# Cross-attention's keys computed in the mixer's end, and its values with the memory's tokens on partitions

## The chip, the cores and the metric

The kernel runs on one NeuronCore of one Trainium2 chip. The metric is the time of one execution on the device in microseconds (us). The program holds TensorE (PE; its weight loads are listed apart as PEld), VectorE (DVE), ScalarE (ACT), a little GpSimd (POOL), and DMA transfers that the SyncE queue (SP) issues.

## The reference

A decoder trunk of two layers, sequence 512, width 1024, with a memory of 256 tokens. Each layer adds to `h` in turn: half a SwiGLU feed-forward; a mixer of 8 stick-breaking heads (width 64) and 4 gated delta-rule heads (width 128) with one input and one output projection; a read of the memory; and half a SwiGLU again. The change touches the end of the mixer and the read of the memory:

```python
def memory_cross_attention(xn, memn, w_q, w_kv, w_o):
    q = (xn @ w_q).reshape(B, S, 4, 256)
    k, v = jnp.split(memn @ w_kv, 2, axis=-1)      # memn: 256 x 1024
    ...
    s = jnp.einsum('bshd,bmhd->bhsm', q, k) * (256 ** -0.5)
    p = jax.nn.softmax(s, axis=-1)
    o = jnp.einsum('bhsm,bmhd->bshd', p, v).reshape(B, S, D)
    return o @ w_o
```

`memn` is `rms_norm(mem, mem_norm[l])`: the memory is the same in both layers, only the gain differs. The keys and values therefore depend on nothing that the layer computes.

## The kernel before

All activations lie transposed, with 128 features on the partitions and 512 tokens (for the memory 256) along a row. Every dense product is made from three fp32r matmuls: an operand is split into a high part (a cast on ACT, `split_act`, L170) and a low part (a subtraction on DVE, `split_low`, L176), and `mm3` (L234) issues high x high, high x low and low x high. One matmul here includes its weight load.

**Weights.** A weight block is 128 output features by 1024 inputs, 512 KB. `load` (L179) brings it into one of three raw buffers over SP's queue, `unit` (L186) splits it into one of four pairs of buffers (`W_BUFS`). `self.plan` is the list of blocks in the order in which they are used, `xattn_plan` (L1280) and its like write it, and `take` (L211) takes the next and has the ones after it loaded and split ahead, as far as the four buffers go. `products` (L239) multiplies a block with an operand in eight steps, a `yield` after each.

**Order.** The order of TensorE's instructions is written by hand: stages are Python generators that `weave` (L92) runs against a planned clock. `self.clk` grows with each matmul by its planned time, a `yield 1200.0` says that the thread's next step is due 1200 ns later, and `yield ("q3",)` that it waits for a mark set by another thread. Of the threads that are due, the first in the list goes on. Waits at this level only set the order; on the chip an instruction waits for the data that it needs. The other engines' order comes from a scheduler that also goes by the program's order and by priorities.

**The mixer** (L1150) weaves four threads: the norm's statistics, the delta-rule heads one after another (`mixer_gdn`, `gdn_head` L966), the stick-breaking pairs one after another (`mixer_sb`, `sb_pair` L827), and the dense products (`mixer_dense`, L1183), which fill in wherever no chain step is due. A delta-rule head is a chain of small matmuls, each followed by a DVE step: seven levels of a triangular inverse (their masked product on DVE is L1079, their updates L1084 and L1088), then four chunks of the state (DVE at L1102, L1108, L1118). The dense thread makes the projections of all heads, then four blocks for the gate `z` (L1207 to L1209), then the output projection `project_out` (L690): its first two pairs of blocks take the first four operands (the stick-breaking pairs, `turned`), the fourth of which waits for `sb3`, the last pair's end; then `gated` (L1218) transposes the delta-rule heads' outputs and multiplies them with the gate, and the remaining steps follow.

**The cross-attention** (`xattn`, L1284) loads the memory (`load_mem`, L1258), scales and splits it (`mem_operands`, L1265), and weaves the norm, the heads, and `xattn_dense` (L1291): 8 key blocks, 8 value blocks, 8 query blocks, then the output projection. A key or value block is 24 matmuls with 128 output features on the partitions and 256 tokens along the row. The keys are multiplied by the memory's rms factor along the row (`self.mb`, L1300). The attention needs the values with tokens on the partitions, so each value block is multiplied (L1316), transposed by two TensorE transposes, and copied by ACT (L1307).

Of the kernel before, what the change touches and what calls it, by code (L numbers as in the profile page):

```python
# [30 lines left out]
KD = D // P  # L31
# [16 lines left out]
G_F1, G_MX, G_XA, G_ME, G_F2, G_SB, G_GD, G_CV, G_AL, G_DT, G_LAYER = (  # L48
    0, 8, 16, 24, 32, 40, 44, 45, 93, 97, 101)
# [3 lines left out]
class Trunk:  # L53
# [125 lines left out]
    def load(self, src):  # L179

        raw = self.wpool.tile([P, KD * P], F32, tag="wraw", name=self.name("wraw"), bufs=3)
        raw = raw[:, :src.shape[1]]
        self.nc.sync.dma_start(raw, src)
        return raw
# [781 lines left out]
    def gdn_head(self, layer, head):  # L966
        nc = self.nc
# [4 lines left out]
        q, k, v = self.qkv[head]  # L972
# [102 lines left out]
        for n in range(len(small), len(LEVELS)):  # L1075
            yield 500.0 if n > len(small) else 3300.0
            b = gd()
            each(b, lt, Y)
            tt(v3(U), v3(b), many(mask(n)), op=ALU.mult)  # L1079
            yield 1200.0  # L1080
            if n < len(LEVELS) - 1:
                b = gd()
                each(b, X, U)
                tt(Y, Y, b, op=ALU.subtract)  # L1084
                yield 0
            b = gd()
            each(b, U, X)
            tt(X, X, b, op=ALU.subtract)  # L1088
        rho = self.rsqrt_log(sq4, NT, "rq")
        nc.vector.tensor_scalar(out=rho, in0=rho, scalar1=P ** -0.5, scalar2=None, op0=ALU.mult)  # L1090

# [47 lines left out]
        on = self.on[head] = self.slot(f"s{4 + head}")  # L1139
        tt(v3(on), v3(o), wide(ro), op=ALU.mult)  # L1140
        self.mark(f"g{head}", 5400.0)

    @staticmethod
    def mixer_plan(wi, wo):
# [38 lines left out]
    def mixer_dense(self, layer, x):  # L1183
        nc = self.nc
        wg = self.gate_weights(layer)
        early = yield from self.products(1, x, self.AT[:1])
        b = self.bank("dense", self.AT[1:2])
        for k, (xh, xl) in enumerate(x):
            parts = [(b[:16, :], wg[:, k, :], xh), (b[:8, :], wg[:, k, 0:8], xl)]
            for i, (o, l, r) in enumerate(parts if k == 0 else parts[::-1]):  # L1190
                self.mm(o, l, r, start=k + i == 0, stop=True, skip_group_check=k + i > 0)
            yield 200.0
        self.ab16 = self.slot("s14", shape=(16, S))
        nc.scalar.copy(self.ab16, b[:16, :])
        early.append((yield from self.project(x)))
        yield ("rb",)
        self.mark("ab")
        for p in range(4):
            if p >= 2:
                yield (f"q{p - 2}",)  # L1200
            yield from self.gdn_project(layer, p, x, early if p == 0 else [])
            if p >= 2:
                yield (f"qk{p - 2}",)
            yield from self.sb_project(p, x)
        yield ("qk2",)
        z = self.sb([P, 4, S], "qk", bufs=2)
        for p in range(4):  # L1207
            ps = yield from self.project(x)
            nc.vector.tensor_tensor(z[:, p, :], ps, self.rb, op=ALU.mult)  # L1209
        last = nc.scalar.activation(z, z, AF.Silu)  # L1210
        self.exp_set(last)
        ops = []

        def turned(p):
            yield (f"sb{p}",)
            ops.append(self.to_x(p, self.sbo[p]))

        def gated():  # L1218
            for p in range(4):
                yield (f"g{p}",)  # L1220
                b = self.bank("gate", ("b4", "b5"))
                self.transposes(b, self.on[p])
                t = self.slot(self.turn("gz", ("s12", "s2")))
                nc.vector.scalar_tensor_tensor(out=t, in0=b, scalar=self.gain(layer, G_GD),
                                               in1=z[:, p, :], op0=ALU.mult, op1=ALU.mult)
                ops.append(self.to_x(4 + p, t))

        yield from self.project_out(ops, [turned(p) for p in range(4)], "sb3", gated())


    def mem_norm(self):

        nc = self.nc
        yield ("last",)
        acc = self.cv[:, 4:]
        for i in range(4):
            t = self.slot(("s33", "s6")[i % 2])
            nc.sync.dma_start(t.rearrange("p (k m) -> p k m", k=2), self.a["memT"][:, 2 * i:2 * i + 2, :])
            dst = t if i else acc
            nc.scalar.activation(dst, t, AF.Square)  # L1240
            if i:
                nc.vector.tensor_tensor(acc, acc, t, op=ALU.add)
# [8 lines left out]
        mt = self.rsqrt(ms, 2, "mn")  # L1251
# [6 lines left out]
    def load_mem(self):  # L1258
        mem = self.sb([P, 4, S], "qk", bufs=2)
        for i in range(4):  # L1260
            self.nc.sync.dma_start(mem[:, i, :].rearrange("p (k m) -> p k m", k=2),
                                     self.a["memT"][:, 2 * i:2 * i + 2, :])
        return mem

    def mem_operands(self, layer):  # L1265
        nc = self.nc
        mem = self.load_mem()
        x = []
        for k in range(KD):
            if k % 2 == 0:  # L1270
                mh, ml = self.slot(f"s{k // 2}", F32R), self.slot(f"s{4 + k // 2}", F32R)
            cs = slice((k % 2) * M, (k % 2 + 1) * M)
            g = self.gain(layer, G_ME, k)
            nc.scalar.activation(mh[:, cs], mem[:, k // 2, cs], AF.Copy, scale=g)
            nc.vector.scalar_tensor_tensor(out=ml[:, cs], in0=mem[:, k // 2, cs], scalar=g,
                                           in1=mh[:, cs].bitcast(F32), op0=ALU.mult, op1=ALU.subtract)
            x.append((mh[:, cs], ml[:, cs]))
        return x

    @staticmethod  # L1280
    def xattn_plan(wq, wkv, wo):
        return [*(wkv[i] for i in range(2 * KD)), *(wq[i] for i in range(KD)), *(wo[i] for i in range(KD))]

    def xattn(self, layer):  # L1284
        self.begin()
        mem = self.mem_operands(layer)
        x = self.norm(layer, G_XA, ("s24", "s25", "s26"))
        self.kt, self.vm, self.q, self.xo = {}, {}, {}, []
        self.weave(self.rms(self.GD, 8000.0, 9000.0), self.xattn_heads(), self.xattn_dense(mem, x))

    def xattn_dense(self, mem, x):  # L1291

        nc = self.nc
        kv4 = self.sb([P, 4, S], "qk", bufs=2)
        room = [self.slot(f"s{i}") for i in (34, 35, 36)] + [kv4[:, i, :] for i in range(4)] + [self.slot("s39")]
        for i in range(KD):
            if i % 2 == 0:
                kt = self.kt[i // 2] = room[i // 2]
            ps = yield from self.project(mem, M, self.MM + self.AT[:2])
            nc.vector.tensor_tensor(kt[:, (i % 2) * M:(i % 2 + 1) * M], ps[:, :M], self.mb, op=ALU.mult)  # L1300
        vf = None

        def turned(i, vf):
            b = self.bank("turn", ("b4", "b5"))
            self.transposes(b, vf, n=2)
            dst = self.vm[i // 2].rearrange("p (m d) -> p m d", m=2)[:, :, (i % 2) * P:(i % 2 + 1) * P]
            nc.scalar.copy(dst, b[:, :M].rearrange("p (m d) -> p m d", m=2))  # L1307

        for i in range(KD):
            if i % 2 == 0:  # L1310
                self.vm[i // 2] = room[4 + i // 2]
            ps = yield from self.project(mem, M, self.MM + self.AT[:2])
            if i:
                turned(i - 1, vf)
            vf = self.slot(self.turn("vf", ("s31", "s32")))
            nc.vector.tensor_tensor(vf[:, :M], ps[:, :M], self.mb, op=ALU.mult)  # L1316
        for i in range(KD):
            if i >= 4 and i % 2 == 0:
                yield (f"sc{i // 2 - 2}",)
            ps = yield from self.project(x, banks=(("b0", "b7", "b1")[i % 3],))  # L1320
            if i == 0:
                turned(KD - 1, vf)
# [179 lines left out]
```

## Time and profile before

| | |
|---|---|
| median of 3 runs | 2451.75 us (2449.06 to 2458.12) |
| the profiled execution | 2449.16 us |
| its span in the profile | 2447.3 us |
| TensorE busy, share of the span | 2389.6 us, 98% |
| VectorE busy | 1774.0 us, 72% |
| ScalarE busy | 1184.8 us, 48% |
| mean DMA rate | 90 GB/s |
| TensorE's granted clock, mean | 0.994 |

Busy times overlap, since the engines work side by side. TensorE's matmuls are pipelined and their ends are modelled, so the distance from one matmul's start to the next one's is the better measure of what one costs; a row of the timeline that says `x16` holds sixteen of them. "Idle before <- releaser" is the time in which an engine stood still before a group of instructions, and the instruction whose end let it go on. PEclk is the share of TensorE's full clock (2.4 GHz) that was granted; 0.5 is 1.2 GHz.

In layer 0 of the profiled execution the mixer's gate blocks end at about 630 us, its output projection's remaining steps run from 665 to 710 us, the cross-attention's keys and values from 710 to 759 us; layer 1 follows the same course some 1210 us later.

### The profile page before, as it was taken

The numbers are of one execution on the slowest core, as the hardware profiler recorded it, in microseconds if no ns is written. First come the engines' busy times: TensorE is split into PE (matmuls) and PEld (weight loads), VectorE is DVE, ScalarE is ACT, GpSimd is POOL, SyncE is SP. The second block draws the span as 40 slices with busy tenths as digits, with TensorE's granted clock in tenths as the row PEclk, the third lists the DMA queues.
The fourth block names the chain that finished last, engine by engine and source line by source line (L and its number), as shares of the span: only waits on it lengthen the run. The fifth ranks groups of instructions, "written<-read, shape, count | busy, mean of one in ns | idle before, by whom it ended". The sixth has DMA issues, their size and how long they took to land.

```text
span 2447.3 us, 36463 instructions
## 1 busy us (share of the span) xinstructions
PE 2389.6 (98%) x14580; PEld 2111.7 (86%) x14580; DVE 1774.0 (72%) x3146; ACT 1184.8 (48%) x2044; POOL 8.1 (0%) x19
## 2 busy tenths in 40 slices
PE   9999999999899999999999999999998999999998
PEld 7999987888689889898889999788886988899997
DVE  7868677888775578585686767598986655777765
ACT  5535355665544445353444444465564444444443
POOL 0000000000000000000000000000000000000000
PEclk9999999999999999999999999999999999999999
DMA  4323242111133123232323232321111422232322
GB/s 160 116 78 128 79 130 69 52 53 52 44 121 121 54 84 114 85 121 87 113 77 121 87 119 80 113 70 44 52 52 36 154 97 76 78 113 86 114 89 82
DMA packets 65273, 220.51 MB, mean 90 GB/s; under 512 B 7376, under 2 KB 10192, under 8 KB 65104
## 3 DMA queue, kind: packets, MB, share of 16 engines
q1 hardware_dynamic: 64672, 217.82, 26.9%
q8 instruction: 114, 1.87, 0.3%
q14 instruction: 55, 0.45, 0.1%
q10 hardware_dynamic: 432, 0.37, 0.1%
HBM read 216.07 MB, written 2.10 MB: 89 GB/s over the span
## 4 chain that ended last, share of the span: by engine, by line
PE 86%; DVE 11%; ACT 1%; issue 1%; DMA 1%; SPq 0%; ACTq 0%; DVEq 0%; POOL 0%
PE b L118 85%; PE b L738 1%; DVE wlo L177 1%; DVE qkv L951 1%; DVE s L865 1%; DVE s L860 1%; ACT whi L172 1%; DVE s L867 0%; DVE s L1079 0%; DVE s L177 0%; DVE s L415 0%; DMA s<-csr 0%; DVE s L1048 0%; DVE s L1088 0%; DMA wraw<-f1i 0%
## 5 line engine op out<-in xcount | busy, mean ns | idle before, releaser
L118 PE MATMUL b<-s,whi 128*128 128x256 f32 (+1 forms) x3064 | 657.3, 305 | 1.8 <-DVE s L459 1.4
L172 ACT CAST whi<-wraw 128x1024 fp32r<-128x1024 f32 (+3 forms) x412 | 387.5, 952 | 495.0 <-PE b L118 452.2
L118 PE MATMUL b<-xh,whi 128*128 128x512 f32 (+1 forms) x1552 | 582.3, 400 | 5.8 <-ACT xh L172 3.0
L118 PE MATMUL b<-xl,whi 128*128 128x512 f32 x1472 | 547.0, 392 | 4.3 <-DVE xl L299 2.4
L177 DVE TENSOR_TENSOR wlo<-wraw,whi 128x1024 fp32r<-128x1024 f32 (+3 forms) x412 | 450.8, 1101 | 123.6 <-ACT whi L172 122.1
L118 PEld LDWEIGHTS b<-s,whi 128*128 128x128 f32 x3064 | 496.9, 190 | 29.2 <-DVE s L459 1.7
L118 PE MATMUL b<-xh,wlo 128*128 128x512 f32 (+1 forms) x1288 | 503.8, 391 | 4.1 <-DVE wlo L177 4.1
L118 PE MATMUL b<-s,wlo 128*128 128x256 f32 (+1 forms) x1532 | 466.8, 305 | 1.1 <-DVE wlo L177 1.1
L118 PEld LDWEIGHTS b<-xh,whi 128*128 128x128 f32 x1552 | 291.8, 189 | 61.1 <-ACT xh L172 4.2
L118 PEld LDWEIGHTS b<-xl,whi 128*128 128x128 f32 x1472 | 277.7, 189 | 59.3 <-DVE xl L177 5.0
L118 PEld LDWEIGHTS b<-s,wlo 128*128 128x128 f32 x1532 | 291.2, 190 | 14.3 <-DVE wlo L177 1.5
L118 PEld LDWEIGHTS b<-xh,wlo 128*128 128x128 f32 x1288 | 242.8, 189 | 58.5 <-DVE wlo L177 6.9
L118 PE MATMUL b<-qk,whi 128*128 128x256 f32 (+1 forms) x1152 | 232.9, 289 | 0.0
L574 DVE SCALAR_TENSOR_TENSOR h<-b,h 128x512 f32<-128x512 f32 (+1 forms) x98 | 66.3, 679 | 176.6 <-PE b L118 176.6
L118 PEld LDWEIGHTS b<-qk,whi 128*128 128x128 f32 x1152 | 180.4, 191 | 2.4
L118 PE MATMUL b<-qk,wlo 128*128 128x256 f32 (+1 forms) x576 | 166.4, 289 | 0.0
L118 PE MATMUL b<-qkv,whi 128*128 128x256 f32 x816 | 160.4, 281 | 0.0
L172 ACT CAST whi<-vv 128x1024 fp32r<-128x1024 f32 x68 | 71.5, 1051 | 133.3 <-issue 71.4
L118 PEld LDWEIGHTS b<-qkv,whi 128*128 128x128 f32 x816 | 126.1, 190 | 0.2 <-ACT s L531 0.2
L118 PE MATMUL b<-qkv,wlo 128*128 128x256 f32 x408 | 114.7, 281 | 0.0
L118 PEld LDWEIGHTS b<-qk,wlo 128*128 128x128 f32 x576 | 110.1, 191 | 1.3
L118 PEld LDWEIGHTS b<-s,s 128*128 128x128 f32 x656 | 83.0, 191 | 25.7 <-DVE s L1079 10.5
(274 smaller groups left out, 3118.0 us busy)
## 6 DMA issues: line engine op xcount, KB each, us to landing
wraw<-f2i SPq DMA_DIRECT2D x88, 512.0 KB, 3.2
wraw<-f1i SPq DMA_DIRECT2D x86, 512.0 KB, 3.2
wraw<-wi SPq DMA_DIRECT2D x56, 512.0 KB, 3.2
wraw<-f1o SPq DMA_DIRECT2D x32, 512.0 KB, 3.5
wraw<-xkv SPq DMA_DIRECT2D x32, 512.0 KB, 3.2
wraw<-f2o SPq DMA_DIRECT2D x32, 512.0 KB, 3.5
wraw<-wo SPq DMA_DIRECT2D x16, 512.0 KB, 3.2
wraw<-xq SPq DMA_DIRECT2D x16, 512.0 KB, 3.3
```

What stands on the lines that cost most here:

```text
L118: self.nc.tensor.matmul(out, lhsT, rhs, **kw)
L172: self.nc.scalar.copy(hi, src)
L177: self.nc.vector.tensor_tensor(lo, src, hi.bitcast(F32), op=ALU.subtract)
L574: stt(out=h, in0=p, scalar=0.5, in1=h, op0=ALU.mult, op1=ALU.add)
L738: self.nc.tensor.transpose(out, src, self.ident[:src.shape[0], :src.shape[0]])
L860: nc.vector.scalar_tensor_tensor(out=t1, in0=z[:, :w], scalar=0.0, in1=t1, op0=ALU.max, op1=ALU.add)
L865: nc.vector.tensor_tensor_scan(out=run[:, back], data0=self.ones[:, 0:1].to_broadcast([P, width]), data1=t1[:, back], initial=0.0, op0=ALU ...
L951: nc.vector.scalar_tensor_tensor(out=y, in0=cv[:, 1 + i:1 + i + S], scalar=w[i], in1=y, op0=ALU.mult, op1=ALU.add)
```

## The change

**Keys.** The 8 key blocks of the weight list are put ahead of the 8 blocks of the mixer's output projection. In `mixer_dense`, four quarters of the memory are loaded one after the other into the one buffer `cv`, the first when `qk2` is marked, and each is scaled and split (`mem_operands(layer, i)`, now one quarter, into room that is free at this point) after a gate block. The last quarter is split after the mark `qk3`. Six of the eight steps of the first two key blocks come before `qk3`; the rest of the key blocks follow, with the operands of the stick-breaking pairs 0 to 2 prepared in between, and the fifth and the seventh block wait, before their result is stored, for the marks `l3` (new: the last head's levels are done) and `q3` (its chunks are done), since they go into buffers that the chain uses until then. Only then does the output projection start. The keys' multiplication and the last quarter's split have high priority with the scheduler.

**Values.** The value weights are the moving operand now and the memory the stationary one: the product comes out with 128 tokens on the partitions and 4 x 128 features along the row, so the transposes and the multiplication ahead of them go. A load fetches 256 inputs of four blocks (runs of 1 KB), and the factor of the rms, now one per partition, goes into ACT's copy.

The core of the diff:

```diff
     def load(self, src):
         raw = self.wpool.tile([P, KD * P], F32, tag="wraw", name=self.name("wraw"), bufs=3)
+        if len(src.shape) == 3:
+            self.nc.sync.dma_start(raw.rearrange("p (i c) -> p i c", i=src.shape[1]), src)
+            return raw
...
+        self.mark(f"l{head}")
         rho = self.rsqrt_log(sq4, NT, "rq")
...
         yield ("qk2",)
+        self.load_mem(0)
         z = self.sb([P, 4, S], "qk", bufs=2)
         for p in range(4):
             ps = yield from self.project(x)
             nc.vector.tensor_tensor(z[:, p, :], ps, self.rb, op=ALU.mult)
+            if p < 3:
+                self.mem_operands(layer, p)
...
-                t = self.slot(self.turn("gz", ("s12", "s2")))
+                t = self.slot(self.turn("gz", ("s2", "s3")))
...
-        yield from self.project_out(ops, [turned(p) for p in range(4)], "sb3", gated())
+        gens = [self.products(1, self.mem, self.MM, M, kn=KD) for _ in range(2)]
+        for gen in gens:
+            for _ in range(KD - 2):
+                next(gen)
+                yield 0
+        yield ("qk3",)
+        with self.tc.high_priority():
+            self.mem_operands(layer, 3)
+        self.kt = {}
+        yield from self.keys(range(2), self.MM, gens)
+        for p in range(3):
+            yield from turned(p)
+        yield from self.keys(range(2, self.KEYS), self.MM, free={4: "l3", 6: "q3"})
+        early = [self.until()] * 3 + [turned(3)]
+        yield from self.project_out(ops, early, "sb3", gated())
...
+    def load_mem(self, i):
+        self.nc.sync.dma_start(self.cv[:, 4:].rearrange("p (k m) -> p k m", k=2),
+                               self.a["memT"][:, 2 * i:2 * i + 2, :])
+
+    def mem_operands(self, layer, i):
...
+        raw = self.cv[:, 4:]
+        mh, ml = self.mem_room[2 * i:2 * i + 2]
+        for j in range(2):
+            cs = slice(j * M, (j + 1) * M)
+            g = self.gain(layer, G_ME, 2 * i + j)
+            nc.scalar.activation(mh[:, cs], raw[:, cs], AF.Copy, scale=g)
+            nc.vector.scalar_tensor_tensor(out=ml[:, cs], in0=raw[:, cs], scalar=g,
                                            in1=mh[:, cs].bitcast(F32), op0=ALU.mult, op1=ALU.subtract)
+            self.mem.append((mh[:, cs], ml[:, cs]))
+        if i < 3:
+            self.load_mem(i + 1)
+
+    def keys(self, blocks, banks, begun=(), free={}):
+        for i in blocks:
+            ps = yield from (begun[i] if i < len(begun) else self.products(1, self.mem, banks, M))
+            if i % 2 == 0:
+                if i in free:
+                    yield (free[i],)
+                self.kt[i // 2] = self.slot(("", "s13", "s34", "s35")[i // 2]) if i else self.cv[:, 4:]
+            with self.tc.high_priority():
+                self.nc.vector.tensor_tensor(self.kt[i // 2][:, (i % 2) * M:(i % 2 + 1) * M], ps[0][:, :M], self.mb,
+                                             op=ALU.mult)
+
+    def xattn_plan(self, wq, wkv, wo):
+        self.plan[-KD:-KD] = [wkv[i] for i in range(self.KEYS)]
+        wv = [wkv[KD + 4 * h:KD + 4 * h + 4, :, 2 * P * i:2 * P * (i + 1)].rearrange("i p c -> p i c")
+              for h in range(2) for i in range(KD // 2)]
+        return [*(wkv[i] for i in range(self.KEYS, KD)), *wv, *(wq[i] for i in range(KD)), *(wo[i] for i in range(KD))]
...
+        yield from self.keys(range(self.KEYS, KD), self.MM + self.AT[:2])
+        for h in range(2):
+            ps = [self.bank("dense", self.MM + self.AT[:2]) for _ in range(2)]
+            for i in range(KD // 2):
+                hi, lo = (t.rearrange("p (i c) -> p i c", i=4) for t in self.take())
+                for k in (2 * i, 2 * i + 1):
+                    cs = slice((k % 2) * P, (k % 2 + 1) * P)
+                    for m, p in enumerate(ps):
+                        ms = slice(m * P, (m + 1) * P)
+                        self.mm3(p.rearrange("p (i c) -> p i c", i=4), (mem[k][0][:, ms], mem[k][1][:, ms]),
+                                 (hi[:, :, cs], lo[:, :, cs]), k == 0, k == KD - 1)
+                    yield 0
+                self.held -= 1
+            for j in range(2):
+                vm = self.vm[2 * h + j] = kv4[:, 2 * h + j, :]
+                for m, p in enumerate(ps):
+                    nc.scalar.activation(vm[:, m * M:(m + 1) * M], p[:, j * M:(j + 1) * M], AF.Copy,
+                                         scale=self.mt[:, m:m + 1])
```

`KEYS` is 8, so all keys are made in the mixer and the `keys` call in the cross-attention makes none. What the values' new loop replaces is the pair of loops of `xattn_dense` over keys and values, with `turned`.

## Rows read from the trace of the kernel before

**Rows 1.** The page: busy time by engine, and the chain that ended last, by engine.
```profile
PE 2389.6 (98%) x14580; PEld 2111.7 (86%) x14580; DVE 1774.0 (72%) x3146; ACT 1184.8 (48%) x2044; POOL 8.1 (0%) x19
...
PE 86%; DVE 11%; ACT 1%; issue 1%; DMA 1%; SPq 0%; ACTq 0%; DVEq 0%; POOL 0%
```
**Rows 2.** Stretches: start:end, length, busy us by engine (instructions), PEclk, DMA share, GB/s.
```profile
core 0: us, PE busy (x) PEld busy (x) DVE busy (x) ACT busy (x) POOL busy (x), PEclk, DMA share, GB/s
570.70:599.50 28.80, 28.26 (x169) 24.39 (x168) 23.99 (x43) 17.38 (x32) 0.00 (x0) 1.00 0.16 56
606.00:636.10 30.10, 28.80 (x168) 23.90 (x168) 25.78 (x54) 20.06 (x33) 0.00 (x0) 1.00 0.15 53
636.10:665.10 29.00, 20.05 (x128) 17.07 (x127) 20.21 (x48) 14.07 (x38) 0.00 (x0) 0.89 0.12 37
665.10:674.00 8.90, 8.88 (x30) 6.88 (x31) 0.69 (x1) 0.00 (x0) 0.00 (x0) 0.78 0.01 2
1846.90:1874.90 28.00, 18.57 (x129) 15.66 (x128) 20.24 (x49) 14.13 (x38) 0.00 (x0) 0.92 0.11 38
...
710.30:759.50 49.20, 49.20 (x415) 49.20 (x416) 33.12 (x54) 23.67 (x32) 0.00 (x0) 1.00 0.50 172
```
**Rows 3.** Timeline of TensorE, mixer's end, layers 0 and 1 (start, us, idle before).
```profile
639.53 1.13 PE L118 MATMUL b<-s,s 128*128 128x128 f32 x8 [0.54 <-DVE s L1073]
641.88 3.10 PE L118 MATMUL b<-s,s 128*128 128x128 f32 x24 [1.22 <-DVE s L1079]
...
662.52 1.09 PE L738 MATMUL b<-cst,s 128*128 128x128 f32 x4 [1.89 <-DVE rot L264]
665.12 0.80 PE L118 MATMUL b<-xh,whi 128*128 128x512 f32 x1 [1.52 <-ACT xh L172]
...
669.26 0.39 PE L118 MATMUL b<-xh,whi 128*128 128x512 f32 x1
...
673.81 0.39 PE L118 MATMUL b<-xh,wlo 128*128 128x512 f32 x1
674.04 1.03 PE L738 MATMUL b<-cst,s 128*128 128x128 f32 x8
...
1874.89 0.80 PE L118 MATMUL b<-xh,whi 128*128 128x512 f32 x1 [1.51 <-ACT xh L172]
...
1884.70 1.03 PE L738 MATMUL b<-cst,s 128*128 128x128 f32 x8
```
**Rows 4.** Timeline of TensorE, mixer, 604.8 to 612.0 us.
```profile
605.13 0.39 PE L118 MATMUL b<-cb 128*128 128x512 bf16 x1
605.42 0.63 PE L738 MATMUL b<-cst,s 128*128 128x128 f32 x4
...
609.91 1.95 PE L118 MATMUL b<-qkv 128*128 128x128 f32 x16
611.69 0.22 PE L118 MATMUL b<-cb 128*128 128x128 bf16 x1
```
**Rows 5.** Chain that ended last, in order of time, among the value blocks (start, us).
```profile
741.05 2.87 PE b L118 x24
...
744.14 2.85 PE b L118 x24
```
**Rows 6.** Groups by line and form, 636 to 775 us (busy, mean ns, idle before).
```profile
L177 DVE TENSOR_TENSOR wlo<-wraw,whi 128x1024 fp32r<-128x1024 f32 x26 | 31.5, 1222 | 14.8 <-ACT whi L172 14.8
L172 ACT CAST whi<-wraw 128x1024 fp32r<-128x1024 f32 x26 | 26.9, 1050 | 43.5 <-PE b L118 42.2 <-issue 1.3
...
L1274 ACT ACTIVATE s<-qk,gn 128x256 fp32r<-128x256 f32 x8 | 3.6, 501 | 3.7 <-DMA qk<-memT 2.7 <-DVE xl L177 1.0
L1275 DVE SCALAR_TENSOR_TENSOR s<-qk,gn,s 128x256 fp32r<-128x256 f32 x8 | 3.5, 476 | 0.0
...
L1300 DVE TENSOR_TENSOR s<-b,mb 128x256 f32<-128x256 f32 x6 | 2.5, 422 | 0.8 <-PE b L118 0.8
L1307 ACT COPY qk<-b 128x256 f32<-128x256 f32 x6 | 2.2, 366 | 0.0
```
**Rows 7.** DMA issues, 636 to 646 us (KB each, us to landing).
```profile
qk<-memT SPq DMA_DIRECT2D x4, 256.0 KB, 5.2
```

More of the change, by code (lines that the diff above doesn't have):

```diff
@@ L1141, in gdn_head @@
         self.mark(f"g{head}", 5400.0)
+    KEYS = 8
     @staticmethod
@@ L1250, in mem_norm @@
                                 op0=ALU.mult, op1=ALU.add)
-        mt = self.rsqrt(ms, 2, "mn")
+        mt = self.mt = self.rsqrt(ms, 2, "mn")
         yield 7000.0
@@ L1256, in mem_norm @@
         nc.scalar.copy(self.mb, b[:, :M])
[L1258 to L1265, printed above, removed]
-        nc = self.nc
[L1267 to L1275, printed above, removed]
-                                           in1=mh[:, cs].bitcast(F32), op0=ALU.mult, op1=ALU.subtract)
-            x.append((mh[:, cs], ml[:, cs]))
-        return x
@@ L1280, in xattn_plan @@
-    @staticmethod
-    def xattn_plan(wq, wkv, wo):
-        return [*(wkv[i] for i in range(2 * KD)), *(wq[i] for i in range(KD)), *(wo[i] for i in range(KD))]
+    def load_mem(self, i):
+        self.nc.sync.dma_start(self.cv[:, 4:].rearrange("p (k m) -> p k m", k=2),
+                               self.a["memT"][:, 2 * i:2 * i + 2, :])
+    def mem_operands(self, layer, i):
+        nc = self.nc
+        if i == 0:
+            t = self.sb([P, 3, S], "qkv", F32R, bufs=2)
+            self.mem = []
+            self.mem_room = [t[:, 0, :], t[:, 1, :], t[:, 2, :], self.sb([P, S], "vl", F32R),
+                             self.sb([P, S], "ml", F32R), self.slot("s12", F32R)]
+        if i == 3:
+            self.mem_room += [self.slot("s14", F32R), self.sb([P, 4, S], "qk", F32R, bufs=2)[:, 0, :]]
+        raw = self.cv[:, 4:]
[5 more added lines that the diff above has]
+            nc.vector.scalar_tensor_tensor(out=ml[:, cs], in0=raw[:, cs], scalar=g,
+                                           in1=mh[:, cs].bitcast(F32), op0=ALU.mult, op1=ALU.subtract)
+            self.mem.append((mh[:, cs], ml[:, cs]))
+        if i < 3:
+            self.load_mem(i + 1)
@@ L1284, in xattn @@
+    def xattn_plan(self, wq, wkv, wo):
[3 more added lines that the diff above has]
+        return [*(wkv[i] for i in range(self.KEYS, KD)), *wv, *(wq[i] for i in range(KD)), *(wo[i] for i in range(KD))]
     def xattn(self, layer):
         self.begin()
-        mem = self.mem_operands(layer)
         x = self.norm(layer, G_XA, ("s24", "s25", "s26"))
-        self.kt, self.vm, self.q, self.xo = {}, {}, {}, []
@@ L1289, in xattn @@
-        self.weave(self.rms(self.GD, 8000.0, 9000.0), self.xattn_heads(), self.xattn_dense(mem, x))
+        self.vm, self.q, self.xo = {}, {}, []
+        self.weave(self.rms(self.GD, 8000.0, 9000.0), self.xattn_heads(), self.xattn_dense(self.mem, x))
     def xattn_dense(self, mem, x):
@@ L1294, in xattn_dense @@
         kv4 = self.sb([P, 4, S], "qk", bufs=2)
[L1295 to L1316, printed above, removed]
+        yield from self.keys(range(self.KEYS, KD), self.MM + self.AT[:2])
[16 more added lines that the diff above has]
+                                         scale=self.mt[:, m:m + 1])
         for i in range(KD):
@@ L1320, in xattn_dense @@
             ps = yield from self.project(x, banks=(("b0", "b7", "b1")[i % 3],))
-            if i == 0:
-                turned(KD - 1, vf)
             j = i % 4
```

## The prediction

> **What bounds the kernel now.** I read the page first: TensorE is busy 98% of the span and carries 86% of the chain of work that ended last [rows 1], so time is saved only by giving TensorE less to do or by filling its gaps. Then the stretches: TensorE, VectorE (DVE) and granted clock around the places that the diff touches [rows 2]. In the middle of the mixer (570.70 to 599.50) TensorE is busy 28.26 of 28.80 us. In the mixer's end (636.10 to 665.10) it is busy 20.05 of 29.00 us, and the granted clock falls to 0.89 there and to 0.78 in the 8.9 us behind it; layer 1 shows the same at 1846.90. The cross-attention's keys and values (710.30 to 759.50) fill TensorE wholly. Third, the timeline of TensorE in the mixer's end [rows 3]: from 636.10 on nothing is left for it but the steps of the last delta-rule head and the last stick-breaking pair, each waiting for DVE, until the fourth step of the output projection starts at 665.12.
>
> How much of the 29.0 us is real work? Busy time does not tell, since ends are modelled. The stretch holds 128 matmuls [rows 2]; 88 of them are 128x128 in fp32, and sixteen of those in a row take 1.78 us from start to start [rows 4], 0.111 each; the rest run from 2 to 512 columns, and I take the same mean. That is 14.2 us of work and **14.8 us of gaps**; in layer 1 28.0 less 14.2, 13.8 us. After the gaps TensorE runs at 1.2 GHz: the 30 matmuls of 512 columns from 665.12 to 674.04 take 8.92 us, where at 2.4 GHz a matmul takes 0.2275 us (20 from 669.26 to 673.81 [rows 3]), 6.83 us in all. So the low clock costs 2.1 us in layer 0. Layer 1's thirty take from 1874.89 to 1884.70, 9.81 us [rows 3], so 3.0 us. A perfect filler could win 16.9 and 16.8 us.
>
> **The change, part by part**, each per layer.
>
> Keys. 8 blocks of 24 matmuls of 256 columns leave the cross-attention for the mixer's end. 24 of them take 2.87 us [rows 5], 0.1195 each: 192 cost 22.9 us, out of a place where TensorE is full, into one that can absorb up to 16.8 us.
>
> Values. 192 matmuls of 256 columns (22.9 us) and 16 transposes (a block repeats after 3.09 us and its matmuls take 2.87 [rows 5], so 0.22 for two, 1.7 us in all) go. In come 96 matmuls of 512 columns, two weight loads where there were four: 96 x 0.2275 = 21.8 us. That wins 2.8 us.
>
> At the row the price of a weight load shows nowhere: 256 columns at 2.4 GHz alone are 0.107 us, and load and matmul together repeat after 0.1195 [rows 5]. The Trainium skill, "TensorE: Matmul & The Clock Gate", Part 3, The mechanism, has weight loads overlap running matmuls only in other row groups, and its section LDWEIGHTS prices one at columns over 1.2, here 107 ns; by that, 96 loads fewer would win about 10 us more in each layer, an estimate from that page. The trace disagrees, and the sum goes by the rows.
>
> New in the values: the moving operand is read in four runs of 128 columns, 256 apart. The trace of before shows no such fp32r matmul. Nearest rows: contiguous, 0.2275; and the mask row of the delta rule, a bf16 operand read four times over in runs of 128, which takes 0.29 us until the next starts [rows 4], some of it a change of type. I take 0.2275 (the output stays contiguous and each run is long) and keep 0.29, 6 us a layer, as the upper end; a gain is excluded, since nothing runs faster than contiguous.
>
> Other engines, in the mixer's end. DVE gets 8 splits of a weight block (1.22 us each), 8 multiplications of the keys (0.42) and 8 splits of the memory (0.48) [rows 6]: 17 us; ACT 8 casts of a block (1.05) and 8 of the memory (0.50): 12.4 us. Six of the eight memory splits lie in the z stage, where DVE is busy 25.78 of 30.10 us [rows 2], so 2.9 us just fit; the rest, 14 us, goes to the tail, where DVE has 20.2 of 29.0 us and almost nothing in the 9 us after. About 35 us of DVE work in some 44 us is 79%; in the mixer's middle it lives with 24.0 of 28.8 us, 83% [rows 2]. So DVE is not the bound by amount, but the chain's steps queue behind 1.22 us splits. In the middle that costs TensorE 0.5 us in 28.8 [rows 2], with fillers of three matmuls of 512 columns, 0.68 us; the keys' steps are 0.36 us, so a chain's step comes up sooner and waits oftener. Ends: 0.5 us a layer (as in the middle) and 9.8 (all eight splits land in the chain's way). I take 3.5, nearer the middle, whose mix it is.
>
> DMAs. Four loads of the memory (256 KB, 5.2 us to land [rows 7]) move to the z stage, into a single buffer, so SP stops at each until the quarter before it is split; queued behind it are weight loads. Three raw buffers and four split ones cover it, 5.5 us of z matmuls (24 x 0.2275) each; without that cover a load costs its 5.2 us. The value weights come in runs of 1 KB where it was 4 KB; the stretch uses half the DMA engines' time [rows 2], and blocks are loaded ahead during the output projection. Both at nothing, and the POOL queue is not touched.
>
> New waits. "qk3", "l3" and "q3" stop only the dense thread, which holds nothing else then; by the planner's own times it has keys left at each of them (about 15 us of filler fit between z and "q3"). In the values, one counter hands out the four banks: in layer 0 the second half gets b0 and b1, and the first query block needs b0, which waits for three copies of 0.37 us [rows 6] and a hand-over, about 1.4 us, after 0.3 at the start; in layer 1 the first value block waits 0.9 us for the projection's last bank. 1.2 a layer, between 0 and 1.7. The scaling of the values moves from DVE to the copies on ACT, which were there before: nothing.
>
> **The sum**, two layers: 45.8 (keys, in) - 45.8 (keys, out) - 5.6 (values) - 33.7 (gaps and clock filled) + 7.0 (steps that wait) + 2.4 (banks) = -29.9. Check by stretch: out of the cross-attention go 22.9 + 2.8 = 25.7 us a layer, into the mixer's end come 22.9 - 16.8 + 3.5 = 9.6. The profiled execution took 2449.16 us, so 2419.3; the median run is 2.6 above it, so 2421.9, and I say **2421**. Lower end: 1.0 for the steps, no banks: -38.3, 2411 on the profiled scale. Upper end: 19.6 for the steps and 3.4: -16.3, 2433.
>
> **The rivals.** (1) DVE's queue stretches the chains: all splits in the way, 2433, 2435 on the median's scale. For it: DVE is at 86% in the z stage [rows 2]. Against: the middle's small loss.
> (2) The change doesn't do what it says: the keys come behind the chains rather than between their steps, because their units or the memory's last quarter are late. Then the gaps stay and only the values' gain remains: -5.6 + 2.4, 2446, 2449 by the median: no difference. For it: the second key block's end needs the memory's last quarter, which waits for pair 3's scores. Against: six of its eight steps don't.
> (3) Slower: the strided moving operand runs at half rate, 0.455 us. Then 192 matmuls cost 43.7 us more: 2463, 2465.6 by the median. It decides from 0.2275 + 29.9 / 192 = 0.383 us on. For it: no row shows this form at full rate. Against: the mask row's 0.29. The Trainium skill, "PSUM — Partial Sum Buffer", Specifications, says of 8-byte cachelines that "any non-contiguous AP slows matmuls significantly"; no run here shows that, and here the operand in SBUF is the broken one, not the output.
>
> **How the numbers follow.** Forecast (2411 to 2431) 0.62; rival 1 0.13; a strided price near 0.29, 12 us, so about 2434, 0.05; rival 2 0.13; rival 3 0.07. The range 2408 to 2438 holds the first three, 0.80. A measurement can tell 0.5%, 12.3 us, here: faster means under 2439.5, slower over 2464. Faster 0.62 + 0.13 + 0.05 = 0.80, no difference 0.13, slower 0.07.
>
> **What would show it.** Right: between 636 and the output projection's fourth step the timeline has 256-column matmuls between the chains' steps, TensorE's waits there under 5 us, a granted clock of 1.00 up to the gates' transposes, which come some 9.6 us later than 674; value matmuls 0.23 us apart; the first query block about 24 us after the output projection ends, not 49. Wrong: key matmuls in a block behind the last chain step; many waits on DVE's L1079 and L1108 kinds of step over 1 us; value matmuls over 0.29 us apart; SP stopped at the memory's loads while a cast waits for its block.

## The result and the profile after

The changed kernel takes 2422.95 us (median of 4 runs, 2421.59 to 2424.92) against 2453.84 us of the kernel before (4 runs beside it), a ratio of 0.9875 [0.9854, 0.9897]. The forecast of 2421 us was 2 us off, inside its range, and the likeliest case came in. The sum behind it was not right in every term, and one term was missing.

The page of the changed kernel has TensorE busy for 13.6 us less than [rows 1] (224 instructions fewer, and fewer of them at the low clock); the other 12 us of the shorter span are idle time.

```profile
PE 2376.0 (98%) x14356; PEld 2094.6 (86%) x14356; DVE 1767.4 (73%) x3130; ACT 1183.4 (49%) x2044; POOL 8.0 (0%) x19
```

The stretches that answer to [rows 2] (start:end, length, busy us by engine, PEclk, DMA share, GB/s): the mixer's end in both layers, the projection's last steps before the gates' transposes, and the values, which now stand alone.

```profile
633.80:676.00 42.20, 40.01 (x327) 38.51 (x326) 35.00 (x69) 24.18 (x45) 0.00 (x0) 1.00 0.25 88
676.00:688.40 12.40, 12.19 (x57) 9.74 (x56) 4.25 (x10) 1.84 (x3) 0.00 (x0) 1.00 0.24 85
...
724.30:748.60 24.30, 24.04 (x112) 19.74 (x112) 17.12 (x29) 14.86 (x24) 0.00 (x0) 1.00 0.54 180
1830.90:1873.00 42.10, 39.91 (x326) 38.43 (x326) 34.89 (x69) 24.11 (x44) 0.00 (x0) 1.00 0.25 89
```

In the mixer's end TensorE was busy 20.05 of 29.00 us at a clock of 0.89 [rows 2]; now it is busy 40.01 of 42.20 at 1.00, and the stretch behind it is at 1.00 too, where it was 0.78. The timeline of TensorE shows how (start, us, idle before; `ml`, `s`, `qk` against `whi` and `wlo` in 256 columns are key steps):

```profile
637.04 1.10 PE L118 MATMUL b<-s,s 128*128 128x64 f32 x8 [0.51 <-DVE s L1051]
...
638.43 0.28 PE L118 MATMUL b<-ml,whi 128*128 128x256 f32 x1
...
645.77 0.50 PE L118 MATMUL b<-qkv,whi 128*128 128x256 f32 x2 [0.57 <-DVE cv L1318]
646.11 0.28 PE L118 MATMUL b<-qkv,wlo 128*128 128x256 f32 x1
646.23 1.06 PE L118 MATMUL b<-s,s 128*128 128x128 f32 x8
...
688.46 1.04 PE L741 MATMUL b<-cst,s 128*128 128x128 f32 x8
```

Where [rows 3] had a chain step, a wait of 0.5 to 1.9 us and the next chain step, key steps now stand between. TensorE's waits from the first key step to the gates' transposes (688.46) are four, 2.2 us in all.

The price of the change, by stage (us; the first key step, and before the first step of the output projection at 629.27 and 1840.07, ends the gate stage):

| stage | before, layers 0 and 1 | after | difference | by the sum |
|---|---|---|---|---|
| head 3's start to the end of the gate blocks | 28.93, 28.96 | 31.83, 30.24 | +2.9, +1.3 | 0 |
| to the gates' transposes | 44.77, 44.63 | 54.65, 54.60 | +9.9, +10.0 | +9.6 |
| rest of the output projection | 36.23, 36.24 | 35.91, 35.90 | -0.3, -0.3 | 0 |
| keys and values, to the first query block | 49.03, 49.03 | 24.28, 23.9 | -24.8, -25.1 | -24.5 |

That is -12.3 and -14.1 where the sum had some -14.9 in each. The profiled executions differ by 25.55 us (2449.16 and 2423.61), since the stages outside the table are 0.85 us longer: in the changed kernel's execution the clock is low for a while from 531.5 us on, at the start of layer 0's head 2, which costs 1.4 us there; two other profiled executions of the kernel lack it. The medians differ by more, 30.89 us, since the execution of before that was profiled was among the fastest of its runs.

**The term that was missing** is in the first line: head 3's start. DVE's timeline there and TensorE's (the changed kernel, same columns):

```profile
605.91 0.48 DVE L1304 SCALAR_TENSOR_TENSOR vl<-cv,gn,qkv 128x256 fp32r<-128x256 f32 x1
...
606.46 0.48 DVE L1304 SCALAR_TENSOR_TENSOR vl<-cv,gn,qkv 128x256 fp32r<-128x256 f32 x1
...
607.53 0.16 DVE L1008 TENSOR_TENSOR sc<-sc,beta 128x4 f32<-128x4 f32 x1
...
608.53 0.68 DVE L1019 TENSOR_TENSOR s<-s,sc 128x512 f32<-128x512 f32 x1
609.13 0.74 DVE L938 SCALAR_TENSOR_TENSOR s<-s,gn,b 128x512 f32<-128x512 f32 x1
```

```profile
607.77 0.63 PE L741 MATMUL b<-cst,s 128*128 128x128 f32 x4 [0.59 <-DVE sc L1008]
609.93 1.06 PE L741 MATMUL b<-cst,s 128*128 128x128 f32 x4 [1.53 <-DVE s L938]
...
611.86 0.63 PE L118 MATMUL b<-xh,whi 128*128 128x512 f32 x1
612.28 0.63 PE L118 MATMUL b<-xl,whi 128*128 128x512 f32 x1
...
613.77 0.39 PE L118 MATMUL b<-xh,whi 128*128 128x512 f32 x1
614.00 0.40 PE L118 MATMUL b<-xl,whi 128*128 128x512 f32 x1
```

The same place in the kernel before (L935 and L1016 there are L938 and L1019 here):

```profile
606.19 0.74 DVE L935 SCALAR_TENSOR_TENSOR s<-s,gn,b 128x512 f32<-128x512 f32 x1
606.84 0.68 DVE L1016 TENSOR_TENSOR s<-s,sc 128x512 f32<-128x512 f32 x1
```

```profile
606.98 0.66 PE L738 MATMUL b<-cst,s 128*128 128x128 f32 x4 [0.93 <-DVE s L935]
```

TensorE waits 2.1 us there where it waited 0.93 before, in two parts. Two splits of the memory (0.48 us each) stand in DVE's queue ahead of the short steps up to L1008: 0.59 us. And the scheduler has put L1019 ahead of L938, on which TensorE waits, where it stood behind it before: another 0.60 us. In layer 0 the clock falls behind the wait: the granted clock is 0.68 from 608.50 to 613.80, 512 columns take 0.43 us from start to start (611.86 to 612.28) and then 0.23 again, and the stage loses another 1.6 us. The same happened in layer 1, not in layer 0, in other executions, and in neither layer in some (last section).

### The profile page after: what moved, and what is told of

Same layout as the page of the kernel before. It is cut to its first block, busy times and chain, and to the rows that moved or that the text cites. A ratio compares the mean times of both kernels' runs of the same rounds, so it can differ in the third digit from the quotient of the medians.

```text
span 2421.8 us, 35988 instructions
## 1 busy us (share of the span) xinstructions
PE 2376.0 (98%) x14356; PEld 2094.6 (86%) x14356; DVE 1767.4 (73%) x3130; ACT 1183.4 (49%) x2044; POOL 8.0 (0%) x19
## 4 chain that ended last, share of the span: by engine, by line
PE 85%; DVE 11%; ACT 2%; issue 1%; DMA 1%; SPq 0%; ACTq 0%; POOL 0%; DVEq 0%
PE b L118 84%; DVE wlo L177 2%; PE b L741 1%; DVE qkv L954 1%; DVE s L868 1%; ACT whi L172 1%; DVE s L863 1%; DVE s L870 1%; DVE s L177 0%; DVE s L1082 0%; DVE s L1051 0%; DMA s<-csr 0%; DVE s L418 0%; DMA wraw<-f1i 0%; DVE s L1087 0%
## 5 line engine op out<-in xcount | busy, mean ns | idle before, releaser
L118 PE MATMUL b<-s,whi 128*128 128x256 f32 (+1 forms) x2616 | 582.1, 309 | 1.4 <-DVE s L462 1.4
L118 PEld LDWEIGHTS b<-s,whi 128*128 128x128 f32 x2616 | 430.0, 190 | 28.0 <-DVE s L462 1.7
L118 PE MATMUL b<-s,wlo 128*128 128x256 f32 (+1 forms) x1308 | 403.5, 309 | 1.1 <-DVE wlo L177 1.1
L118 PEld LDWEIGHTS b<-s,wlo 128*128 128x128 f32 x1308 | 248.6, 190 | 14.3 <-DVE wlo L177 1.5
L118 PE MATMUL b<-qk,whi 128*128 128x256 f32 (+1 forms) x1184 | 241.9, 289 | 0.0
L118 PEld LDWEIGHTS b<-qk,whi 128*128 128x128 f32 x1184 | 186.5, 191 | 2.4
L118 PE MATMUL b<-qkv,whi 128*128 128x256 f32 x912 | 183.0, 283 | 1.2 <-DVE cv L1318 1.1
L118 PEld LDWEIGHTS b<-qkv,whi 128*128 128x128 f32 x912 | 142.1, 190 | 1.8 <-DVE cv L1318 1.6
L118 PE MATMUL b<-qkv,wlo 128*128 128x256 f32 x472 | 132.7, 281 | 0.0
```

The costliest lines, as they stand in the source:

```text
L118: self.nc.tensor.matmul(out, lhsT, rhs, **kw)
```

## The experiments

Each kernel is an edit of the changed one. H is the time from head 3's start to the gates' transposes, layers 0 and 1 of the profiled execution: 73.70 and 73.59 before, 86.48 and 84.84 in the changed kernel. Kernels named together ran on the same chip.

**Keys in one block behind the chains** (with the next three; before: 2452.89).

```diff
+        yield ("sb3",)
         gens = [self.products(1, self.mem, self.MM, M, kn=KD) for _ in range(2)]
```

> The changed kernel, but the key blocks wait until the stick-breaking pairs are done, so that they run as one block behind the chains. Theory (the gain is the gaps between the chain's steps, filled): the gaps of some 14 us a layer and the low clock stay, and the 18 output-projection matmuls that used to run ahead of them (4.1 us a layer) move behind them too. Against the kernel before: values -4 us, those 8 us added, so about 2458 where the kernel before takes 2454, and over 30 us more than the changed kernel; TensorE's waits in the mixer's end over 7 us a layer again. Rival (the gain lies in where the weights and the memory are prepared, not in the interleaving): within 8 us of the changed kernel, 2423 to 2431.

Measured: 2458.25 us, 1.0017 [1.0006, 1.0028] of before; H is 100.79 in layer 0. Its stretches in layer 0, the chains and then the keys:

```profile
632.50:668.20 35.70, 26.27 (x154) 22.49 (x153) 24.87 (x52) 18.30 (x38) 0.00 (x0) 0.85 0.07 24
668.20:690.00 21.80, 21.80 (x172) 21.79 (x171) 13.24 (x24) 7.99 (x13) 0.00 (x0) 0.93 0.39 121
```

With the same work and another place for the key steps, the gaps and the low clock are back and some 35 us are lost: the gain is the filling. This is what rival 2 would have looked like; the prediction put it at 2449, without the price of the memory's preparation, which the next kernel shows, and without that of the projection's 18 matmuls that now follow the chains too (4.1 us a layer by the expectation).

**The values alone**: the keys back in the cross-attention, the memory still prepared in the mixer.

```diff
-    KEYS = 8
+    KEYS = 0
...
-        gens = [self.products(1, self.mem, self.MM, M, kn=KD) for _ in range(2)]
...
+        yield from self.project_out(ops, [turned(p) for p in range(4)], "sb3", gated())
...
         self.begin()
+        self.mem_operands(layer, 3)
```

> Only the values are new; the keys stay in the cross-attention, and of the memory's four quarters the first three are still prepared between the gate blocks. Theory: the values win 2.8 us a layer by the sum and about 2 by the changed kernel's trace, so 4 us in all, near 2450 where the kernel before takes 2454. Rival (the values' new form is worth much of the change, since transposes, weight loads and work on DVE go): 10 us or more, 2444 or less.

Measured: 2452.84 us, 1.0001 [0.9991, 1.0011]: no gain, where 2450 was expected. The keys' and values' stretch is 47.2 us instead of 49.03, but H is 76.15 and 76.41, 2.5 and 2.8 more than before:

```profile
606.00:637.70 31.70, 29.20 (x171) 24.22 (x171) 28.77 (x76) 21.25 (x53) 0.00 (x0) 1.00 0.21 67
637.70:682.00 44.30, 34.34 (x186) 28.05 (x186) 25.24 (x57) 16.37 (x37) 0.00 (x0) 0.88 0.04 13
...
717.90:765.10 47.20, 46.98 (x304) 42.65 (x304) 30.27 (x46) 23.96 (x32) 0.00 (x0) 1.00 0.55 178
```

DVE is busy 28.77 of 31.70 us in the first row, and TensorE waits 0.6 us on L1008 and 1.5 us on L938 as in the changed kernel, so the gate stage is 1.3 us longer. What costs the rest, behind it, was not tried apart. Preparing the memory in the mixer thus takes back what the new values win.

**The keys alone**: the values in their old form.

```diff
-        wv = [wkv[KD + 4 * h:KD + 4 * h + 4, :, 2 * P * i:2 * P * (i + 1)].rearrange("i p c -> p i c")
-              for h in range(2) for i in range(KD // 2)]
+        wv = [wkv[KD + i] for i in range(KD)]
...
+            ps = yield from self.project(mem, M, self.MM + self.AT[:2])
+            if i:
+                turned(i - 1, vf)
+            vf = self.slot(self.turn("vf", ("s31", "s32")))
+            nc.vector.tensor_tensor(vf[:, :M], ps[:, :M], self.mb, op=ALU.mult)
...
```

> Only the keys move; the values are made as before, with features on the partitions, multiplied on DVE and transposed. Theory: the keys alone bring the gain less the values' 4 us, so 2427 where the changed kernel takes 2423. Rival (keys and values help each other, for instance because the values' DVE work would collide with what the mixer's end leaves behind): less than the difference, 2432 or more.

Measured: 2429.38 us, 0.9905 [0.9889, 0.9921]; H is 84.88 and 84.87. The values run from the first to the last of these rows, 26.23 us, against 24.28 in the changed kernel:

```profile
723.27 0.47 PE L118 MATMUL b<-qkv,whi 128*128 128x256 f32 x2 [0.19 <-ACT whi L172]
...
749.50 0.48 PE L118 MATMUL b<-xh,whi 128*128 128x512 f32 x1
```

The keys bring 23.5 us alone; the new values bring 2.0 a layer on top by the trace, 6.4 us by the medians of different chips, which differ by up to 3.9 us for the changed kernel itself (below).

**Longer key steps**, six matmuls instead of three, fewer changes between chain and keys.

```diff
-                yield 0
+                if k % every == every - 1:
+                    yield 0
...
-        gens = [self.products(1, self.mem, self.MM, M, kn=KD) for _ in range(2)]
+        gens = [self.products(1, self.mem, self.MM, M, kn=KD, every=2) for _ in range(2)]
...
```

> The changed kernel with key steps of six matmuls (0.72 us) instead of three (0.36 us). Theory (steps that come up too soon wait for DVE, and each return from a chain's matmul to a key's costs some 0.06 us): half the returns and fewer waits, 1 to 3 us less in all, 2420 to 2422. Rival (a chain step that is due waits behind six matmuls, and the chain gets longer): 1 to 3 us more. Third: within 1 us, then neither matters.

Measured: 2426.03 us (2423.94 to 2427.41), 0.9889 [0.9875, 0.9904], H 85.24 and 85.23. Not faster, against the theory; H is 0.4 us longer than the changed kernel's 84.84, which points to the rival, but the medians are of different chips. One wait has come up that the changed kernel lacks:

```profile
PE b L118 <- DVE yv L1113: 1.3, 1, 1.3
```

**The changed kernel again** (with the next three; before: 2452.65).

> The changed kernel itself, unedited, on the same chip as the three runs beside it, so that differences of 1 to 3 us can be read: about 2423, 30 us under the kernel before.

Measured: 2423.07 us (2422.17 to 2424.19), 0.9878 [0.9863, 0.9893].

**Six key blocks in the mixer**, the last two in the cross-attention: `KEYS = 6`.

> Six key blocks in the mixer's end, two in the cross-attention. Theory (the end of the mixer absorbs 16.8 us a layer, about six blocks; the last two only displace what TensorE would do anyway): within 2 us of the changed kernel. Rival (the stretch still has room for the last blocks, waits or low clock come back without them): 3 to 8 us slower. Third (each block there costs waits and returns, so fewer are better): 1 to 3 us faster.

Measured: 2431.57 us (2429.76 to 2434.14), 8.5 slower than the changed kernel. H is 82.85 in layer 0: only 2.0 us shorter without two blocks that take 5.7. TensorE's timeline at the end of the chains:

```profile
673.31 0.49 PE L118 MATMUL b<-yv,s 128*128 128x128 f32 x2 [0.38 <-DVE yv L1112]
...
675.95 0.49 PE L118 MATMUL b<-xh,whi 128*128 128x512 f32 x1 [1.49 <-ACT xh L172]
676.67 0.50 PE L118 MATMUL b<-xl,whi 128*128 128x512 f32 x1 [0.23 <-DVE xl L177]
...
678.86 0.63 PE L118 MATMUL b<-xh,wlo 128*128 128x512 f32 x1
```

The last two blocks cover 2.1 us of waits on the last chunk and the last operand, and the low clock that follows them (0.63 long rows at 678.86; 0.88 granted from 676 to 690). So the theory, that six blocks fill the stretch, was wrong, and the rival came.

**The memory's quarters one gate block later.**

```diff
-            if p < 3:
-                self.mem_operands(layer, p)
+            if p:
+                self.mem_operands(layer, p - 1)
```

> The memory's first three quarters are scaled and split one gate block later each (after the second, third and fourth instead of the first, second and third). Theory: their DVE work at the last head's start, on a DVE that is 86% busy there, is what makes TensorE wait 2.1 us on L1008 and L938 where it waited 0.9 before; moved away, the waits go back to 0.9, 2 to 3 us less in both layers together, about 2420.5. Rival (the waits only move, to the levels of the inverse or to the first key blocks, which need the third quarter): within 1 us, or slower.

Measured: 2423.39 us (2422.29 to 2424.01), no change. It tells little: the trace has the splits of the second quarter at 604.74 and 605.29, 3.9 us after head 3's start as in the changed kernel (605.91 less 601.98). The scheduler kept them at the same place in DVE's queue; the edit did not move what it was to move.

**The key blocks' low parts on GpSimd.**

```diff
+        if pool:
+            self.nc.gpsimd.tensor_tensor(lo[:, :n], raw, hi[:, :n].bitcast(F32), op=ALU.subtract)
+        else:
+            self.split_low(lo[:, :n], raw, hi[:, :n])
...
```

> The low parts of the key blocks are subtracted on POOL, which is idle, instead of on DVE. Theory (what is left of waits in the mixer's end, 2.2 us a layer, comes from chain steps queued behind 1.2 us splits on DVE): 2 to 4 us less, about 2420. Rival (the order of the steps sets the waits, DVE has room): within 1 us. Third (POOL is much slower at it, over 2.9 us a block, the pace at which a block is used): the key blocks come late and the stretch grows, 5 us or more slower.

Measured: 2430.44 us (2429.32 to 2432.65), 7.4 slower. DVE is relieved (30.25 busy us from 634 to 676, 34.83 in the changed kernel), but a split takes twice DVE's 1.22:

```profile
L197 POOL TENSOR_TENSOR wlo<-wraw,whi 128x1024 fp32r<-128x1024 f32 x16 | 39.9, 2500 | 620.9 <-DVE mo L1145 538.5 <-ACT whi L173 82.4
```

H is 88.04 and 89.70. The gate stage is 2.1 us longer in both layers than in the changed kernel with the same clock. No run takes the causes apart, but the trace shows that DVE itself is held up. This short step, which takes 0.16 us in the changed kernel, takes 1.34 us and ends with POOL's split:

```profile
601.43 2.37 POOL L197 TENSOR_TENSOR wlo<-wraw,whi 128x1024 fp32r<-128x1024 f32 x1 [269.46 <-DVE mo L1145]
```

```profile
602.48 1.34 DVE L272 TENSOR_TENSOR rot<-roy 128x4 f32<-128x4 f32 x1 [1.05 <-ACT roy L271]
```

Five such DVE steps in each layer overlap a split on POOL and end at or up to 0.8 us behind its end; in layer 0 they take 7.1 us longer in all than in the changed kernel. Neither the theory nor the third case (POOL over 2.9 us a block) had this.

**The splits held back behind their gate block** (with the next two; before: 2454.45).

```diff
-            nc.vector.tensor_tensor(z[:, p, :], ps, self.rb, op=ALU.mult)
-            if p < 3:
+            zi = nc.vector.tensor_tensor(z[:, p, :], ps, self.rb, op=ALU.mult)
+            if p in (1, 2):
+                with self.after(zi):
+                    self.mem_operands(layer, p)
+            elif p < 3:
                 self.mem_operands(layer, p)
```

> The changed kernel with the second and third quarter of the memory split after the multiplication of their own z block, so that no split stands in DVE's queue between the normalisation of head 3 and the transposes that wait for it (TensorE's order is the same). Theory: those splits, which I had costed at nothing, make TensorE wait 2.1 us at head 3's start where it waited 0.9 before; held back, the waits return to about 0.9 and the kernel gains 1.2 us a layer: about 2420.6 us against 2423.0, and the z stage shortens by 1.2. Rival: the waits only move to a later step of the z stage (z stage as long as before): 2423. Second rival: the later loads make the first key blocks wait for the third quarter: 2425 or more.

**Its measure, the changed kernel once more.**

> The changed kernel unedited, as the measure for the two beside it: 2423 us, within 1.5.

Measured: 2420.30 us (2419.96 to 2425.04) held back, 0.9870 [0.9854, 0.9887] of before; 2426.83 us (2423.76 to 2430.33) for the changed kernel beside it, 0.9892 [0.9876, 0.9908]. H with the splits held back is 83.92 in both layers; unedited it is 84.90 and 86.49. Waits of TensorE from 600 to 700 us, and the stages, with the splits held back (its lines after L1217 are three further on):

```profile
PE b L118 <- DVE s L1051: 1.2, 2, 0.7
PE b L118 <- DVE cv L1321: 0.9, 1, 0.9
PE b L741 <- DVE s L938: 0.9, 1, 0.9
```

```profile
601.10:630.80 29.70, 28.08 (x169) 23.68 (x169) 26.83 (x71) 19.55 (x51) 0.00 (x0) 1.00 0.22 71
630.80:685.00 54.20, 51.95 (x383) 48.24 (x382) 39.65 (x79) 26.32 (x48) 0.00 (x0) 1.00 0.27 88
```

The order of TensorE's instructions is the same, so the difference is DVE's queue: no split stands ahead of L1008, and L938 is ahead of L1019 again. The wait at L938 is 0.9 again, L1008's is gone, and the rival has a part too: L1051's 0.5 has become 1.2. The gate stage gains 0.6 us, half of the 1.2 expected, the end 0.4, and the clock does not fall at this place. The changed kernel's median here is 3.8 us above what it took on the two other chips. This is the fastest kernel of the study by its median. The intervals against before overlap with the changed kernel's; that it is faster rests on H in both layers of one execution each.

**The key blocks' low parts computed twice** on DVE.

```diff
-        self.split_low(lo[:, :n], raw, hi[:, :n])
+        for _ in range(2 if twice else 1):
+            self.split_low(lo[:, :n], raw, hi[:, :n])
...
```

> The changed kernel with the low part of each key block's weights computed twice on DVE: 8 x 1.22 = 9.8 us more of DVE in each layer, between the start of head 3 and the end of the mixer, TensorE's work unchanged. Theory (DVE is not the bound by amount, but the chains' steps queue behind these splits): some third of it shows, 3 us a layer, 2429 us. Rival 1 of the prediction (the splits stand in the chains' way one for one): 9.8 a layer, 2443. Other rival (DVE's 17% of idle time in the tail takes them all): 2423.

Measured: 2439.34 us (2436.32 to 2440.47), 0.9941 [0.9926, 0.9955]: 12.5 slower than the changed kernel beside it, 16.3 slower than where that ran before. H is 92.35 and 92.38, 7.5 more than the undisturbed 84.84. Of 9.8 us more work on DVE 7.5 show, where a third was expected. DVE's timeline where the longest wait (4.70 us) arises, at L178, the line of `split_low` here:

```profile
660.04 4.62 DVE L178 TENSOR_TENSOR wlo<-wraw,whi 128x1024 fp32r<-128x1024 f32 x4
664.57 1.61 DVE L178 TENSOR_TENSOR s<-b,s 128x512 fp32r<-128x512 f32 x3
```

Four weight splits in a row stand ahead of three that the last stick-breaking pair needs. This is rival 1's mechanism. A part of the 7.5 us is the clock behind that wait (0.92 granted from 632.86 to 675.00). The changed kernel, with DVE busy 83% of its end, pays 2.2 us of waits a layer for it and has little room left: of further work on DVE some two thirds (medians, same chip) to three quarters (H) show.

## Why the prediction was right, and where not

**The number: partly luck.** On its own scale, that of the profiled executions, the sum's 2419.3 was 4.3 us too low (2423.61): the term below that was missing makes 2.6 of it, the low clock behind head 3's wait 1.6, and the other differences nearly cancel. The median still came within 2 us of 2421, because the medians differ by 5.3 us more than the profiled executions; the sum has no term for that. Other executions of before are longer at a lower mean clock (2450.00 us at 0.994 and 2457.99 at 0.990, beside the first experiment), and those of the changed kernel spread less.

**Keys in, gaps and clock filled: right.** The stretch to the gates' transposes grew by 9.9 and 10.0 us, predicted 9.6. With 22.9 in and 16.9 and 16.8 filled, "steps that wait" cost 3.9, taken as 3.5. The four waits make 2.2 of them. Another 1.4 was not thought of: behind narrow chain steps the first matmul of a key step costs more, 0.20 us from start to start instead of 0.12 behind fp32 steps of 128 or fewer columns (second pair of rows), 0.17 behind fp32r ones of 128 columns (first pair). Of 24 returns from the chains a layer, 19 meet this. So 3.5 came out near, though the waits that it meant were 2.2.

```profile
643.56 0.33 PE L118 MATMUL b<-s,whi 128*128 128x256 f32 x1
643.73 0.28 PE L118 MATMUL b<-qk,whi 128*128 128x256 f32 x1
...
651.07 0.36 PE L118 MATMUL b<-ml,whi 128*128 128x256 f32 x1
651.27 0.28 PE L118 MATMUL b<-s,whi 128*128 128x256 f32 x1
```

Putting the keys behind the chains gave the gaps back (H 100.79), so the filling is shown, not only argued. Layer 0's granted clock is 1.00 from 633.80 to 688.40, as the prediction asked for.

**The memory's splits in the gate stage: wrong.** "So 2.9 us just fit", from 25.78 busy of 30.10 us, took a sum of time for a place in the queue. The row it read also starts at 606.00, 5.7 us behind head 3's start at 600.34. In the stretch that matters, the kernel before had DVE busy for 4.03 of 4.10 us:

```profile
602.90:607.00 4.10, 3.17 (x17) 2.18 (x15) 4.03 (x17) 2.12 (x9) 0.00 (x0) 1.00 0.40 128
```

The 2.9 us fit into the stage, but two of the six splits landed in the few microseconds in which TensorE has used up its filler and waits for a row of short DVE steps, whose order changed too. It cost 1.3 us a layer, and in some executions 1.6 more in a layer in which the clock fell. The values-only kernel has the same waits without the keys, and holding the splits back lowers the price. Had this term stood in the sum, the forecast would have been some 2.6 us higher (2423.6).

**Values: right, with the banks.** The sum had -2.8 and +1.2, so -1.6; the traces of the kernels with the old and the new values differ by 2.0 in the stretch. The banks' waits were smaller: the first query block waited 0.25 us instead of 1.4.

**Strided operand (rival 3): refuted.** The value matmuls and the first query block, changed kernel:

```profile
732.94 0.40 PE L118 MATMUL b<-wlo,s 128*128 128x512 f32 x1
733.17 0.40 PE L118 MATMUL b<-whi,qk 128*128 128x512 f32 x1
733.41 0.39 PE L118 MATMUL b<-whi,s 128*128 128x512 f32 x1
...
748.65 0.50 PE L118 MATMUL b<-xh,whi 128*128 128x512 f32 x1 [0.25 <-ACT qk L1356]
```

They start 0.23 to 0.24 us apart, as contiguous ones do (0.2275 [rows 3]), and the whole stretch takes 24.3 us. The Trainium skill, "PSUM — Partial Sum Buffer", Specifications, warns of PSUM that a non-contiguous access slows matmuls; for an SBUF operand in runs of 128 columns of 4 bytes no run here shows it. By the Trainium skill, "TensorE: Matmul & The Clock Gate", Part 3, The mechanism, a weight load overlaps matmuls only in other row groups; with the price of its section LDWEIGHTS, the 96 loads fewer would have shown as about 10 us a layer, an estimate from that page. The trace disagrees here too, since the values gained 2.0.

**Rival 1** did not come, but its mechanism is real: doubled splits cost 7.5 of 9.8 us more a layer. **Rival 2** did not come: the key steps do stand between the chain's steps.

**DMAs: right.** The memory's quarters landed in 2.4 us, the value weights with their 1 KB runs in 4.3 (4 KB runs: 3.2 in the mixer, 3.6 for the query weights beside them); the first values waited 0.19 us for a cast. Rows of DMA issues, 585 to 660 us and 690 to 750 us:

```profile
wraw<-xkv SPq DMA_DIRECT2D x8, 512.0 KB, 3.2
...
cv<-memT SPq DMA_DIRECT2D x3, 256.0 KB, 2.4
...
wraw<-xkv SPq DMA_DIRECT2D x8, 512.0 KB, 4.3
```

## What to carry to other kernels

Independent work that sits where the bound engine is full is worth moving into a chain's gaps, and the trace prices it well: real work in the gap, plus what the clock loses behind it, less a few tenths per step that comes late. Filler needs operands, though, and preparing them on the engine that feeds the chain is costed by its place in the queue, not by the sum of free time; look at the few instructions on which the bound engine waits, read the busy share of just that stretch, and keep the preparation out from between them. In a stage with the feeding engine at 83%, 7.5 of 9.8 us of further work on it showed.

## What the runs showed of the hardware

TensorE's clock can fall behind a wait, but not in every execution. Nine profiled executions share head 3's start with its waits of 0.6 and 1.5 us (the changed kernel three times, and the edits one block, values alone, keys alone, longer steps, six blocks, quarters later). In 5 of their 18 layers the granted clock falls to 0.5, 1.2 GHz, behind the second wait, and the gate stage takes 31.8 us instead of 30.3. The executions of before and of the kernel with the splits held back, with 0.9 us there, show no fall at this place. The length of the wait does not decide it alone: with the splits computed twice it is 2.1 us, and the clock stays at 1.00 there in both layers. At head 2's start the clock falls in five of the thirteen executions, in one layer each, behind waits of 0.54 and 0.50 us that the others have too without a fall. What decides stays open; shown is the cost, 1.6 us at head 3's start and 1.0 to 3.1 us at head 2's.

The first key matmul of 256 columns behind narrow matmuls takes longer from start to start: 0.20 us behind fp32 ones of 128 or fewer columns, 0.17 behind fp32r ones of 128, 0.12 behind fp32r ones of 256 or more. Whether the change of type makes the difference between 0.20 and 0.17 is not shown.

GpSimd took 2.50 us for the split that takes DVE 1.22, and a DVE step of 0.16 us that overlapped one took 1.34.
